# Decays that carry the key factors in the exponent, chunks inverted in batches of four and six, and merges in three groups

## The chip, the cores and the metric

The kernel runs on one core of one Trainium2 chip. A core has TensorE (PE in the profile), VectorE (DVE), ScalarE (ACT), GpSimd (POOL) and SyncE (SP), which issues most of the loads and stores; ACT and POOL issue some as well. Each engine works through its own instructions in the order in which they stand. The metric is the time of one execution in microseconds (us), measured on the device, as the median of repeated runs.

## What is computed

The kernel computes one layer of a diffusion block over 256 context tokens and 1024 latent tokens of width 1024: norms with learned modulation, one input projection, two groups of heads, an output projection, and a feed-forward layer. The change lies in the first group, four heads of a gated delta rule, run once forwards and once backwards. What it computes for each chunk of tokens is this part of the reference, cut:

```python
G = jnp.cumsum(gc, axis=-1)
diff = G[..., :, None] - G[..., None, :]
decay = jnp.where(incl, jnp.exp(jnp.where(incl, diff, 0.0)), 0.0)
kb = kc * bc[..., None]
A = jnp.where(strict, jnp.einsum('nbhid,nbhjd->nbhij', kb, kc) * decay, 0.0)
rhs = jnp.concatenate([vc * bc[..., None], kb * jnp.exp(G)[..., None]], axis=-1)
sol = lax.linalg.triangular_solve(A + jnp.eye(CHUNK, dtype=A.dtype), rhs,
                                  left_side=True, lower=True, unit_diagonal=True)
qk = jnp.einsum('nbhid,nbhjd->nbhij', qc, kc) * decay
```

Here g is the log of the decay, `bc` is a sigmoid of a projection (beta), and k has been normalized to length one. A scan over the chunks follows, in which each step uses the solution, `qk` and the state.

## The kernel before

The kernel works with chunks of 128 tokens: ten of them (`TT`), chunks 0 and 1 being context. All matrix products in 32 bits are run as three matmuls of split operands (`whi`, `wlo`, `hhi`, `hlo`). Stages in the order of time:

- Up to about 275 us: modulation, the first token-major projections (`token_major`, whose three matmuls stand at L341 to L343 and are called tm here), and the convolution blocks of k and q (`conv_block`, L576 to L578).
- The decay stage, about 280 to 363 us: `pre(t)` for each chunk. PE makes the products of keys with keys (`kk`, L665) and with queries (`kq`, L675) and transposes the queries (`qt`, L670); ACT squares the transposed queries for their norms (L672). For each of the two directions a row of cumulated decays is loaded over all partitions (`gw`, L678). POOL adds a column to each head's 128x128 block (`e`, L683, with `nG`, the negated cumulated decay), and replaces what lies on the wrong side of the diagonal (L685). ACT takes the exponential of all four heads at once (L687). DVE multiplies `kk` and `kq` by it and by a column `ab`, which is beta over the squared key norm, head by head (`ut`, L695; `sp`, L697). `ut` is stored to DRAM (`un`), `sp` as well. `gw` has two buffers, `e` two, `sp` two, `ut` two. Convolution blocks of V fill PE in between.
- V's transposes (`vT`, L820), from which ACT makes scaled copies (`vt`, L823, one buffer) and stores them (ACT's own DMA queue), 12 stores in all.
- `invert(b)`: for the chunks of batch b, the 32x32 diagonal blocks of the triangular matrices are loaded one block to a partition (`yr`), and inverted by DVE in 31 steps of two instructions (L730, L732); the result is transposed (`XT`, L734) and stored (`xd`, L736). The batches are `[0,1,2,9]`, `[3,8,4,7]` and `[5,6]`.
- `merge(b)`: builds the inverse of the whole 128x128 matrix from its blocks. `blocks(b)` loads `un` to a tile `U` (L747), and the inverted blocks into `U` (L751) and into `t64` (L752, `t` in the trace). PE then multiplies 32x32 blocks (L771, L778, L781; `m`) and 64x64 blocks (L794, L798). The result is stored for the scan. tm matmuls of three groups (z, rq, rk) lie between these steps.
- From 582 us: the rest of the scan with the retention heads, the output projection (to about 735 us), and the feed-forward layer.

The order of each engine's instructions is set before the kernel runs, by a scheduler that simulates times and takes ready instructions by a priority, which goes by the place in the code; so one engine's order mixes stages. What SP issues is in one line, and an instruction in it that waits holds up all behind it. Tiles live in pools: a pool that is opened where another was closed uses its memory and waits for its last readers. The pool `rp` of the tile `rope` lies where `cv`, the pool of V's convolution, was:

```python
        close(CV)
        checkpoint("v")
        RP = pool("rp", side="right")
        rope = RP.tile([P, TT, P], F32, tag="rope", name="rope")
        GM = pool("gm")
        for t in BATCH[2]:
            pre(t)
        checkpoint("pre2")
        merge(0)
        SY.dma_start(rope, ap["rope"])
```

## Time and profile before

| | |
|---|---|
| median of 3 runs | 1484.18 us (1483.59 to 1484.78) |
| the profiled execution's own time | 1486.29 us |
| its span, first to last instruction | 1484.5 us |
| mean granted clock of TensorE | 0.977 of full speed |
| PE busy | 1406.9 us, 95% |
| DVE busy | 974.2 us, 66% |
| POOL busy | 628.4 us, 42% |
| ACT busy | 604.9 us, 41% |

The shares are means over stages with different limits, so that a stage has to be looked at by itself. A row of a window gives each engine's busy time in a stretch. The granted clock is a mean over the stretch of two levels, 2.4 GHz (1.00) and 1.2 GHz. Matmul durations in the trace overlap: of back-to-back matmuls the distance between their starts tells what one costs.

### The profile page before, as it was taken

The page shows a single profiled execution, that of the slowest core. Times are in us where ns is not written, and L with a number is a line of the kernel's source. Part 1 is how long each engine was busy: PE and PEld are TensorE (multiplying, and loading weights), DVE is VectorE, ACT ScalarE, POOL GpSimd, SP SyncE. Part 2 cuts the span into 40 slices and gives each one's busy share as a digit, 9 for nine tenths or more (in the row PEclk, how much of TensorE's full clock was granted, in tenths as well). Part 3 has the DMA queues.
Part 4 walks back from the last instruction along what each step waited for, and adds up shares of the span by engine and source line. Part 5 has one row for each costly group of instructions (what it writes and reads, how often), then busy time and mean ns, then how long its engine had stood idle before and what let it go on. Part 6 is the DMA issues. An engine that isn't in the chain of part 4 may idle for free.

```text
span 1484.5 us, 24226 instructions
## 1 busy us (share of the span) xinstructions
PE 1406.9 (95%) x8919; PEld 1206.4 (81%) x8919; DVE 974.2 (66%) x1938; ACT 604.9 (41%) x1268; POOL 628.4 (42%) x581
## 2 busy tenths in 40 slices
PE   7999999987988899999799899999999999999997
PEld 2798888976878899999688688777888888788886
DVE  6566788269868345689767876656555555657486
ACT  5543564375541121245534533323333333444454
POOL 0120011377124343234134689899555553335321
PEclk9999999998999899999899999999999999999999
DMA  8536686578597755996633265765222242776863
GB/s 321 208 99 212 188 250 202 165 233 273 175 266 204 248 186 205 414 361 221 204 114 114 85 207 215 258 243 183 106 107 107 106 144 79 237 278 190 308 204 114
DMA packets 176567, 298.16 MB, mean 201 GB/s; under 512 B 43496, under 2 KB 93880, under 8 KB 172096
## 3 DMA queue, kind: packets, MB, share of 16 engines
q1 hardware_dynamic: 124896, 253.17, 49.5%
q10 hardware_dynamic: 49072, 35.83, 7.7%
q0 software_dynamic: 2480, 7.60, 1.4%
q8 instruction: 70, 1.15, 0.3%
q14 instruction: 49, 0.40, 0.1%
HBM read 206.60 MB, written 89.96 MB: 200 GB/s over the span
## 4 chain that ended last, share of the span: by engine, by line
PE 42%; POOL 4%; DMA 2%; DVE 1%; issue 1%; ACT 0%; SPq 0%; POOLq 0%; ACTq 0%; DVEq 0%
PE ffn L1306 7%; PE ffn L1305 7%; PE ffn L1304 7%; PE fo L1432 4%; PE fo L1430 4%; PE fo L1431 4%; PE op L1163 2%; PE op L1164 2%; PE op L1165 2%; DMA wd<-tw 1%; POOL ws L1277 1%; POOL tw L1358 1%; POOL tw L1357 1%; DVE wlo L315 1%; POOL tw L1359 0%
## 5 line engine op out<-in xcount | busy, mean ns | idle before, releaser
L341 PE MATMUL tm<-whi,hhi 128*128 128x256 f32 (+1 forms) x704 | 201.1, 289 | 5.6 <-ACT xa L354 1.6
L342 PE MATMUL tm<-wlo,hhi 128*128 128x256 f32 (+1 forms) x704 | 201.3, 288 | 0.6 <-DVE wlo L315 0.6
L343 PE MATMUL tm<-whi,hlo 128*128 128x256 f32 (+1 forms) x704 | 199.2, 287 | 0.0
L341 PEld LDWEIGHTS tm<-whi,hhi 128*128 128x128 f32 x704 | 134.0, 191 | 10.0 <-ACT xa L354 2.4
L1304 PE MATMUL ffn<-t,whi 128*128 128x512 f32 x352 | 137.0, 390 | 2.0 <-ACT whi L314 2.0
L1306 PE MATMUL ffn<-t,wlo 128*128 128x512 f32 x352 | 137.1, 390 | 1.5 <-DVE wlo L315 1.5
L1305 PE MATMUL ffn<-t,whi 128*128 128x512 f32 x352 | 137.0, 389 | 0.0
L314 ACT ACTIVATE whi<-wraw 128x512 fp32r<-128x512 f32 (+2 forms) x98 | 75.2, 771 | 151.4 <-PE ffn L1305 80.5
L342 PEld LDWEIGHTS tm<-wlo,hhi 128*128 128x128 f32 x704 | 134.6, 191 | 1.8 <-DVE wlo L315 1.1
L343 PEld LDWEIGHTS tm<-whi,hlo 128*128 128x128 f32 x704 | 134.1, 192 | 1.8 <-issue 0.9
L314 ACT ACTIVATE whi<-ws 128x512 fp32r<-128x512 f32 x88 | 55.6, 632 | 175.4 <-PE ffn L1305 121.6
L315 DVE TENSOR_TENSOR wlo<-ws,whi 128x512 fp32r<-128x512 f32 x88 | 94.3, 1073 | 47.7 <-ACT whi L314 47.5
L1430 PE MATMUL fo<-whi,ahi 128*128 128x512 f32 x308 | 119.3, 390 | 1.3 <-ACT ahi L314 1.3
L1431 PE MATMUL fo<-wlo,ahi 128*128 128x512 f32 x308 | 119.9, 389 | 0.0
L1432 PE MATMUL fo<-whi,alo 128*128 128x512 f32 x308 | 119.0, 390 | 0.0
L315 DVE TENSOR_TENSOR wlo<-wraw,whi 128x512 fp32r<-128x512 f32 (+2 forms) x92 | 100.3, 1092 | 25.0 <-ACT whi L314 25.0
L1304 PE MATMUL ffn<-b,whi 128*128 128x512 f32 x264 | 103.9, 393 | 4.1 <-ACT whi L314 4.1
L1306 PE MATMUL ffn<-b,wlo 128*128 128x512 f32 x264 | 103.9, 394 | 1.1 <-DVE wlo L315 1.1
L1305 PE MATMUL ffn<-b,whi 128*128 128x512 f32 x264 | 103.8, 393 | 0.0
L576 PE MATMUL b<-hhi,whi 128*128 128x512 f32 (+1 forms) x256 | 96.3, 376 | 1.5 <-ACT y L580 1.5
L578 PE MATMUL b<-hhi,wlo 128*128 128x512 f32 (+1 forms) x256 | 95.2, 372 | 0.0
L577 PE MATMUL b<-hlo,whi 128*128 128x512 f32 (+1 forms) x256 | 94.9, 371 | 0.0
(427 smaller groups left out, 3494.6 us busy)
## 6 DMA issues: line engine op xcount, KB each, us to landing
adaw<-ada_w SPq DMA_DIRECT2D x48, 512.0 KB, 4.6
pk<-sd SPq DMA_DIRECT2D x16, 1536.0 KB, 10.1
wraw<-wfi SPq DMA_DIRECT2D x44, 512.0 KB, 4.0
ar<-ad SPq DMA_DIRECT2D x33, 512.0 KB, 4.7
w<-wfo SPq DMA_DIRECT2D x22, 512.0 KB, 4.6
wd<-tw SPq DMA_DIRECT2D x11, 1024.0 KB, 4.8
ad<-act SPq DMA_DIRECT2D x20, 512.0 KB, 3.0
raw<-wd SPq DMA_DIRECT2D x20, 512.0 KB, 4.9
```

What stands on the lines that cost most here:

```text
L314: S.activation(hi, raw, AF.Copy)
L315: e.tensor_tensor(lo, raw, hi.bitcast(F32), ALU.subtract)
L341: T.matmul(o, hhi[:, k, tsl], whi[:, k % 4, :], start=(k == 0), stop=False)
L342: T.matmul(o, hhi[:, k, tsl], wlo[:, k % 4, :], start=False, stop=False)
L343: T.matmul(o, hlo[:, k, tsl], whi[:, k % 4, :], start=False, stop=(k == KT - 1))
L576: T.matmul(o, whi[:, k, :], hh, start=(k == 0), stop=False)
L1304: T.matmul(o, whi[:, k, :], xhi(xn, slice(0, 4), k), start=(first and k == 0), stop=False, **kw)
L1305: T.matmul(o, whi[:, k, :], xlo(xn, slice(0, 4), k), start=False, stop=False, **kw)
L1306: T.matmul(o, wlo[:, k, :], xhi(xn, slice(0, 4), k), start=False, stop=(k == 3), **kw)
L1430: T.matmul(po[g][i], ahi[:, ts], whi, start=(j == 0 and not kw), stop=False, **kw)
L1431: T.matmul(po[g][i], ahi[:, ts], wlo, start=False, stop=False, **kw)
L1432: T.matmul(po[g][i], alo[:, ts], whi, start=False, stop=(j == FH - 1), **kw)
```

## The change

Four parts are changed.

1. The exponent. The column that is added to the cumulated decay now contains the log of beta and the negated log of the squared key norm too, so that `ab` is in the exponential. The log of beta comes from `softplus` on twice the width; the log of the key norms from a new function `log` of 22 DVE instructions on 128x40 numbers. POOL's four additions per chunk and direction go: the select reads `gw` itself, and ACT's exponential adds the column as its bias, one head at a time. `ut` and `sp` become one product each over all four heads.
2. The batches are `[0, 1, 2, 9]` and `[3, 8, 4, 7, 5, 6]`. In the second there are 192 blocks, two to a partition on 96 partitions, so that each of the 62 instructions covers twice the elements. `yr`, `L` and `X` have one buffer, and `XT` uses that of `yr`. The loads of `yr` come in eight pieces where there were four.
3. The merges run over chunks 0 to 3 of the first batch, 0 to 2 of the second and 3 to 5 of the second. `U` and `t64` have two buffers; the loads of inverted blocks are 16 pieces a group where there were eight. All ten `pre` stand ahead of V's stage. The pool of `pre` is opened last and closed before the merges' pool opens.
4. The loads of V's convolution weights, their splits and the two evictions of each bank get the priority of the beginning of the decay stage (`mark`), and all four weight splits are on DVE, where two were on POOL.

```diff
+FAR = -1e30
...
+    def as_of(mark):
+
+        return tc.high_priority(offset=tc.cur_priority - mark) if mark is not None else nullcontext()
...
+    def log(pl, x, n, tag):
...
+        V.tensor_scalar(i, x.bitcast(I32), 23, None, ALU.logical_shift_right)
+        V.tensor_copy(e, i)
...
+        for k in (13, 11, 9, 7, 5, 3):
+            V.scalar_tensor_tensor(a, a, 1.0 / k, q, ALU.add, ALU.mult)
+        V.scalar_tensor_tensor(a, a, 1.0, f, ALU.add, ALU.mult)
...
+        V.scalar_tensor_tensor(a, e, 0.693359375, a, ALU.mult, ALU.add)
+        return a
...
-        av = AB.tile([P, TT * 8], F32, tag="av", name="av")
-        V.tensor_tensor(av.rearrange("p (t c) -> p t c", c=8), xa[:, :, 0:8],
-                        bc(small["dtb"], [P, TT, 8], 1), ALU.add)
+        av = AB.tile([P, 2, TT * 8], F32, tag="av", name="av")
+        av3 = av.rearrange("p a (t c) -> p a t c", c=8)
+        V.tensor_tensor(av3[:, 0], xa[:, :, 0:8], bc(small["dtb"], [P, TT, 8], 1), ALU.add)
+        V.tensor_scalar(av3[:, 1], xa[:, :, 8:16], -1.0, None, ALU.mult)
         S.activation(nA, small["alog"], AF.Exp)
         V.tensor_scalar(nA, nA, -1.0, None, ALU.mult)
-        sp = softplus(AB, av, TT * 8, "sp")
+        sp = softplus(AB, av.rearrange("p a n -> p (a n)"), 2 * TT * 8, "sp")
+
+        lnb = GS.tile([P, TT, 2, H], F32, tag="lnb", name="lnb")
+        V.tensor_scalar(lnb.rearrange("p t d h -> p (t d h)"), sp[:, TT * 8:], -1.0, None, ALU.mult)
+        sp = sp[:, :TT * 8]
...
-        def conv_block(b, y, lat):
-
-            whi, wlo = weights(ap["wg"][b], [KT, P], G if b % 2 else V, W, SY if b in (4, 5) else S)
+        def conv_block(b, y, lat, mark=None):
+
+            with as_of(mark):
+                whi, wlo = weights(ap["wg"][b], [KT, P], G if b % 2 and mark is None else V, W, SY if b in (4, 5) else S)
...
-                S.activation(u[:, c0:c0 + n], o, AF.Copy)
-                S.activation(y[:, c0:c0 + n], o, AF.Copy, scale=cw[:, b, 2:3])
+                with as_of(mark):
+                    S.activation(u[:, c0:c0 + n], o, AF.Copy)
+                    S.activation(y[:, c0:c0 + n], o, AF.Copy, scale=cw[:, b, 2:3])
...
+        lnk = log(GS, nkf, TT * H, "ln").rearrange("p (t h) -> p t h", h=H)
+        nG4 = sm["nG"].rearrange("p (t d h) -> p t d h", d=2, h=H)
+        V.tensor_tensor(lnb, lnb, bc(lnk, [P, TT, 2, H], 2), ALU.subtract)
+        V.tensor_tensor(nG4, nG4, lnb, ALU.add)
...
-        GP = pool("gp")
         GU = pool("gu")
         GI = pool("gi")
-
-        BATCH = [[0,1,2,9],[3,8,4,7],[5,6]]
+        GP = pool("gp")
+
+        BATCH = [[0, 1, 2, 9], [3, 8, 4, 7, 5, 6]]
...
                 e = GP.tile([P, H, P], F32, tag="e", name="e", bufs=2)
+                sg = 1 if d == 0 else -1
+                G.affine_select(out=e, in_=gw, compare_op=ALU.is_ge, fill=FAR, base=0,
+                                pattern=[[0, H], [sg, P]], channel_multiplier=-sg)
                 for h in range(H):
                     col = t * 8 + d * 4 + h
-                    G.tensor_scalar(e[:, h, :], gw[:, h, :], sm["nG"][:, col:col + 1], 1.0, ALU.add, ALU.mult)
-                sg = 1 if d == 0 else -1
-                G.affine_select(out=e, in_=e, compare_op=ALU.is_ge, fill=NEG, base=0,
-                                pattern=[[0, H], [sg, P]], channel_multiplier=-sg)
-                S.activation(e, e, AF.Exp)
+                    S.activation(e[:, h, :], e[:, h, :], AF.Exp, bias=sm["nG"][:, col:col + 1])
                 if t >= 2:
                     sp = GP.tile([P, 2, H, P], F32, tag="sp", name="sp", bufs=2)
                 ut = GU.tile([P, H, P], F32, tag="ut", name="ut", bufs=2)
-                for h in range(H):
-                    col = t * 8 + d * 4 + h
-                    hs = slice(h * P, (h + 1) * P)
-                    abc_ = sm["ab"][:, col:col + 1]
-                    V.scalar_tensor_tensor(ut[:, h, :], pk[:, hs], abc_, e[:, h, :], ALU.mult, ALU.mult)
-                    if t >= 2:
-                        V.scalar_tensor_tensor(sp[:, 0, h, :], pq[:, hs], abc_, e[:, h, :], ALU.mult, ALU.mult)
+                V.tensor_tensor(ut.rearrange("p h i -> p (h i)"), pk, e.rearrange("p h i -> p (h i)"), ALU.mult)
+                if t >= 2:
+                    V.tensor_tensor(sp[:, 0].rearrange("p h i -> p (h i)"), pq, e.rearrange("p h i -> p (h i)"), ALU.mult)
                 SY.dma_start(un[b][:, 1 - d, c * H:(c + 1) * H, :], ut)
...
-            nc_ = len(BATCH[b])
-            nu = nc_ * H
-            nb = 4 * nu
+            nb = 4 * len(BATCH[b]) * H
+            two = 2 * nb > P
+            rows, E = (nb, 2) if two else (2 * nb, 1)
             xd = xds[b] = dr.tile([4 * nb, 1024], F32, tag="xd%d" % b, name="xd%d" % b)
-            yr = GI.tile([P, 1024], F32, tag="yr", name="yr", bufs=1)
+            new = lambda tag, n=2048: GI.tile([P, n], F32, tag=tag, name=tag, bufs=1)
+            yr, L, X = new("yr"), new("L"), new("X")
+
+            def part(t, e):
+
+                return t[:nb, e * 1024:e * 1024 + 1024] if two else t[e * nb:(e + 1) * nb, :1024]
+
             for k in range(4):
-                SY.dma_start(yr[k:2 * nb:4].rearrange("r (i j) -> r i j", j=32),
-                             un[b][q32[k]].rearrange("i e u j -> (e u) i j")[:, :, q32[k]])
...
+                for e in range(2):
+                    SY.dma_start(part(yr, e)[k::4].rearrange("r (i j) -> r i j", j=32),
+                                 un[b][q32[k], e].rearrange("i u j -> u i j")[:, :, q32[k]])
...
+            m = lambda t: t[:rows, :E * 1024].rearrange("p (e i j) -> p e i j", e=E, j=32)
             for j in range(31):
                 n = 31 - j
...
+                tmp = GI.tile([P, 512], F32, tag="tmp", name="tmp", bufs=2)
+                sh = [rows, E, n, j + 1]
+                t3 = tmp[:rows, :E * n * (j + 1)].rearrange("p (e i c) -> p e i c", e=E, c=j + 1)
+                V.tensor_tensor(t3, bc(m(L)[:, :, j + 1:, j], sh, 3), bc(m(X)[:, :, j, :j + 1], sh, 2), ALU.mult)
+                xs = m(X)[:, :, j + 1:, :j + 1]
                 V.tensor_tensor(xs, xs, t3, ALU.subtract)
...
+            XT = new("yr")
+            V.tensor_copy(m(XT).rearrange("p e i j -> p (e i) j"), m(X).rearrange("p e i j -> p e j i"))
+            for i, x in enumerate((part(X, 0), part(XT, 1), part(X, 1), part(XT, 0))):
...
-        def blocks(b):
-
-            nu = len(BATCH[b]) * H
-            nb = 4 * nu
-
...
-            uu = GM.tile([P, 2, len(BATCH[b]), H, P], F32, tag="U", name="U%d" % b, bufs=1)
-            SY.dma_start(uu.rearrange("p e c h j -> p e (c h) j"), un[b])
-            tt = GM.tile([P, 2, nu, 64], F32, tag="t64", name="t64", bufs=1)
+        def blocks(b, c0, nc_):
+
+            nu = nc_ * H
+            us = slice(c0 * H, c0 * H + nu)
+            xv = xds[b].rearrange("(s u b) (i j) -> s b i u j", s=4, b=4, j=32)
+            uu = GM.tile([P, 2, nc_, H, P], F32, tag="U", name="U", bufs=2)
+            u4 = uu.rearrange("p e c h j -> p e (c h) j")
+            SY.dma_start(u4, un[b][:, :, us])
+            tt = GM.tile([P, 2, nu, 64], F32, tag="t64", name="t64", bufs=2)
             G.memset(tt, 0.0)
             for k in range(4):
-                SY.dma_start(uu[q32[k]].rearrange("p e c h j -> p (e c h) j")[:, :, q32[k]], blk(xds[b][:2 * nb], k))
-                SY.dma_start(tt[q32[k]].rearrange("p e u j -> p (e u) j")[:, :, (k % 2) * 32:(k % 2) * 32 + 32],
-                             blk(xds[b][2 * nb:], k))
+                for e in range(2):
+                    SY.dma_start(u4[q32[k], e][:, :, q32[k]], xv[e, k][:, us])
+                    SY.dma_start(tt[q32[k], e][:, :, (k % 2) * 32:(k % 2) * 32 + 32], xv[2 + e, k][:, us])
             return uu, [uu[:, 1 - d] for d in range(2)], [tt[:, d] for d in range(2)]
 
-        def merge(b):
-
-            uu, ub, t64 = blocks(b)
-            nu = len(BATCH[b]) * H
+        def merge(b, c0, nc_):
+
+            uu, ub, t64 = blocks(b, c0, nc_)
...
+        mark = tc.cur_priority
         solve(0)
         solve(1)
         for h in range(H):
             y = newy()
-            conv_block(8 + h, y, False)
+            conv_block(8 + h, y, False, mark)
...
+        close(GP)
         GM = pool("gm")
-        for t in BATCH[2]:
-            pre(t)
-        checkpoint("pre2")
-        merge(0)
+        merge(0, 0, 4)
         SY.dma_start(rope, ap["rope"])
-        invert(2)
-        checkpoint("inv2")
-        merge(1)
-        merge(2)
+        merge(1, 0, 3)
+        merge(1, 3, 3)
...
         close(GU)
-        close(GP)
```

In the order of POOL the additions (`TENSOR_SCALAR`, L683) stood between the selects and the products for `sp`. Before, at the beginning of the decay stage:

```order
13 L683 TENSOR_SCALAR e<-gw,nG 128x128 x8
14 L685 AFFINE_SELECT e<-e 128x512 x2
15 L683 TENSOR_SCALAR e<-gw,nG 128x128 x8
16 L685 AFFINE_SELECT e<-e 128x512 x2
17 L683 TENSOR_SCALAR e<-gw,nG 128x128 x8
18 L685 AFFINE_SELECT e<-e 128x512
19 L701 TENSOR_TENSOR sp<-gw,qc 128x512
```

In the changed kernel, at the same place:

```order
14 L728 AFFINE_SELECT e<-gw 128x512 x4
15 L742 TENSOR_TENSOR sp<-gw,qc 128x512 x2
16 L728 AFFINE_SELECT e<-gw 128x512
17 L742 TENSOR_TENSOR sp<-gw,qc 128x512
18 L728 AFFINE_SELECT e<-gw 128x512
19 L742 TENSOR_TENSOR sp<-gw,qc 128x512
```

Only the selects and the products are left there.

On SP, from the store of the first batch's inverted blocks to the loads of the first merge (the numbers in names tell the batches apart: in before `un_2860` is the first, `un_2861` the second, `un_2862` the third). Before:

```order
132 L736 DMA xd_3091<-X 64x1024 x2
133 L736 DMA xd_3091<-XT 64x1024 x2
134 L698 DMA un_2862<-ut 128x512 x2
135 L747 DMA U_4267<-un_2860 128x4096
136 L834 DMA rope<-rope 128x1280
137 L702 DMA sd<-sp 128x1024
138 L752 DMA t_4269<-xd_3091 32x32x32 x2
139 L702 DMA sd<-sp 128x1024
140 L678 DMA gw<-grow_d 128x512
141 L752 DMA t_4269<-xd_3091 32x32x32 x2
142 L751 DMA U_4267<-xd_3091 32x32x32 x2
```

In the changed kernel, where `un_2893` is the second batch's:

```order
139 L782 DMA xd_3078<-X 64x1024 x2
140 L782 DMA xd_3078<-yr 64x1024 x2
141 L764 DMA yr<-un_2893 24x32x32 x8
142 L791 DMA U<-un_2892 128x4096
143 L878 DMA rope<-rope 128x1280
144 L791 DMA U<-un_2893 128x2x1536
145 L797 DMA t_4181<-xd_3078 32x16x32 x8
146 L796 DMA U<-xd_3078 32x16x32 x8
147 L782 DMA xd_3547<-X 96x1024 x2
```

The stores and loads of chunks 5 and 6 (`ut`, `sp`, `gw`) are gone from between; the load of the second group's `U` stands between `rope` and the first merge's `t`.

On PE the first merge ends with 64x64 products, and in before the second merge's first products (32x32) came 126 tm matmuls later. In the changed kernel they follow directly:

```order
2262 L377 MATMUL tm<-whi,hlo 128x256
2263 L843 MATMUL m_4409<-U,xt_4410 64x64 x16
2264 L815 MATMUL m_4471<-t_4453,U 32x32 x48
2265 L375 MATMUL tm<-whi,hhi 128x256
2266 L376 MATMUL tm<-wlo,hhi 128x256
```

The tm matmuls that lay between now stand behind. Ahead of the first merge there are 312 tm matmuls in the changed kernel where there were 360.

## Rows read from the trace of the kernel before

**Rows 1.** Windows: stretch; PE, PEld, DVE, ACT, POOL busy (count); clock, DMA share, GB/s.

```profile
280.00:300.00 20.00, 20.00 (x122) 17.65 (x122) 12.41 (x26) 10.65 (x23) 12.06 (x21) 1.00 0.47 156
300.00:320.00 20.00, 18.75 (x109) 15.90 (x108) 13.94 (x37) 12.90 (x25) 16.70 (x21) 1.00 0.70 243
320.00:340.00 20.00, 16.68 (x85) 14.88 (x84) 16.42 (x44) 14.27 (x33) 15.10 (x22) 0.83 0.85 269
340.00:360.00 20.00, 11.96 (x84) 10.82 (x82) 18.26 (x50) 12.69 (x30) 15.41 (x26) 0.86 0.83 287
360.00:380.00 20.00, 18.23 (x96) 15.34 (x97) 17.96 (x35) 11.51 (x27) 5.86 (x8) 0.80 0.65 175
...
480.00:500.00 20.00, 14.14 (x287) 13.26 (x286) 7.92 (x24) 3.42 (x6) 4.71 (x11) 0.74 0.71 236
```

**Rows 2.** Groups by line and shape, 240 to 520: busy, mean ns | idle before, releasers.

```profile
L683 POOL TENSOR_SCALAR e<-gw,nG 128x128 f32<-128x128 f32 x80 | 37.9, 490 | 55.5 <-DMA gw<-grow_d 20.8 <-DVE ut L695 15.9 <-DVE sp L697 10.9
...
L695 DVE SCALAR_TENSOR_TENSOR ut<-kk,ab,e 128x128 f32<-128x128 f32 x80 | 23.8, 342 | 38.0 <-ACT e L687 38.0
...
L687 ACT ACTIVATE e<-e 128x512 f32<-128x512 f32 x20 | 12.3, 625 | 4.3 <-POOL e L685 4.1
...
L672 ACT ACTIVATE qt<-qt 128x128 f32<-128x128 f32 x32 | 8.5, 265 | 1.6 <-PE qt L670 0.8 <-ACT qt L672 0.2
...
L672 ACT ACTIVATION_READ_ACCUMULATOR qt<-qt 128x1 f32 x32 | 6.2, 193 | 0.0
```

**Rows 3.** Timeline of DVE, 278 to 284: start, duration, instruction, [idle before].

```profile
283.16 1.12 DVE L695 SCALAR_TENSOR_TENSOR ut<-kk,ab,e 128x128 f32<-128x128 f32 x4 [23.70 <-ACT e L687]
```

**Rows 4.** Waits of PE, 275 to 590: total us, times, longest.

```profile
PE m L778 <- DMA U<-xd: 4.0, 2, 3.0
PE m L771 <- DMA t<-xd: 3.9, 3, 2.6
...
PE m L771 <- DMA U<-un: 2.2, 1, 2.2
```

**Rows 5.** Timeline of PE: first kk, two tm, first merge, dense scan.

```profile
281.89 1.05 PE L665 MATMUL kk<-kc 128*128 128x128 f32 x8
...
419.77 0.28 PE L341 MATMUL tm<-whi,hhi 128*128 128x256 f32 x1
419.89 0.28 PE L342 MATMUL tm<-wlo,hhi 128*128 128x256 f32 x1
...
423.64 0.22 PE L771 MATMUL m<-t,U 32*32 32x32 f32 x2 [2.64 <-DMA t<-xd]
...
581.59 0.61 PE L884 MATMUL Tr<-r,pk 128*128 128x128 f32 x4
```

**Rows 6.** Timeline of ACT, 560 to 720, two groups with column operands.

```profile
608.67 2.44 ACT L977 ACTIVATE XI<-dist,lgs 128x128 f32<-128x128 f32 x8
...
657.03 1.65 ACT L1058 ACTIVATE oc<-oc,nm,rry 128x128 f32<-128x128 f32 x4 [0.49 <-DVE nm L1056]
```

**Rows 7.** Timeline of ACT, V's first copies.

```profile
355.41 0.62 ACT L823 ACTIVATE vt<-vT,svy 128x128 f32<-128x128 f32 x2 [0.53 <-PE vT L820]
```

**Rows 8.** Timeline of DVE, end of the third inversion.

```profile
488.66 1.05 DVE L734 COPY XT<-X 64x1024 f32<-64x1024 f32 x1
```

**Rows 9.** Timeline of SP's queue, 385 to 520: start, issue time, DMA.

```profile
415.95 0.33 SPq L834 DMA_DIRECT2D rope<-rope  x1
...
416.86 2.20 SPq L752 DMA_DIRECT2D t<-xd  x2
...
456.62 3.99 SPq L752 DMA_DIRECT2D t<-xd  x4
464.64 0.34 SPq L747 DMA_DIRECT2D U<-un  x1
...
504.02 3.13 SPq L752 DMA_DIRECT2D t<-xd  x4
```

**Rows 10.** DMA issues, 300 to 530: count, KB each, median us to landing.

```profile
U<-un SPq DMA_DIRECT2D x2, 2048.0 KB, 9.6
```

53 lines of the change are left out of this document (30 added, 23 removed).

## The prediction

> **What bounds the kernel now.** I read the windows first: in each stretch of 20 us, how long each engine worked and at what clock TensorE ran [rows 1]. Over the whole span TensorE is busy 1406.9 of 1484.5 us, and the change leaves its matmuls as they are, so what can move is the time in which TensorE waits or runs at a lower clock. Two places lose most of it here. From 300 to 380 TensorE's busy time falls from 20.00 to 11.96 of 20 and the mean granted clock to between 0.80 and 0.86, which is a mix of the 2.4 and the 1.2 GHz level. In these stretches DVE is busy up to 18.26 of 20, POOL 15 to 17, ACT 13 to 14: this is the decay stage, `pre`, in which POOL builds an exponent, ACT takes the exponential, DVE multiplies, and the next chunk waits for the buffers. No engine is full; the ring of three is. The second place is the merges, 420 to 500, where TensorE falls to 14.14 of 20 at a clock of 0.74.
>
> Then I read what these places wait for. In the decay stage DVE's `ut` stands 38.0 us behind ACT's `e`, and POOL's `e` 55.5 us behind loads and DVE [rows 2]; the longest single wait, 23.70 us, is only the stage's beginning [rows 3]. In the merges TensorE waits for DMA: 4.0 us for `U<-xd` and 3.9 for `t<-xd`, among others [rows 4].
>
> Last I read times on the path, as I use them in the sum [rows 5]: the first kk at 281.89, the first merge matmul at 423.64, the first matmul of the dense scan at 581.59. From the first merge to the dense scan are 158.0 us. TensorE's work in it is, counted in the order, 888 tm matmuls at 0.12 us apart (two neighbours stand in the same rows), 106 us, and 25 us of merge and scan matmuls at the intervals that the trace has where nothing waits: 131 us. So 27 us are lost behind the first merge.
>
> **The change, part by part.**
>
> *The exponent.* Of POOL 80 instructions of 490 ns go, 37.9 us [rows 2]; the select stays. Of DVE 144 products of about 342 ns become 36 of 512 columns. Four small ones take 1.37 us, so a wide one is cheaper than that; I count nothing for it, as DVE then waits for ACT more. ACT pays: 20 exponentials of 128x512 at 625 ns become 80 of 128x128, each with the bias in a column. The nearest row of that shape is XI, eight with a column operand in 2.44 us, 0.305 each; the upper bound is `oc` with two column operands, four in 1.65 us, 0.41 each [rows 6]. I take XI, since one column operand is what it has too.
>
> ACT's sum in the stage: 10.65 + 12.90 + 14.27 + 12.69 = 50.5 us from 280 to 360 [rows 1], with eight of the ten chunks. Splitting the exponentials of these eight: 64 x 0.305 - 16 x 0.615 (12.3/20) = +9.7. Chunks 5 and 6, which now stand here as well: 8 squares of 0.265 + 0.193, 16 exponentials of 0.305 and 4 wide ones of 0.625, together 11.1 [rows 2, 6]. That is 71.3 us. The busiest engine of the ring got to 91% (DVE, 340 to 360), ACT to 71% [rows 1]; with POOL gone from the ring I take 88% for ACT, so 81 us. The order puts 20 convolution matmuls behind the first kk that stood ahead of it, so that the stage opens 4.6 us earlier, at about 277, and ends at 358 to 359. Bounds: 71.3 us without a gap, 349; at 71%, 378. Before, the V transposes behind it began a little before the first copy at 355.41 [rows 7]. So the stage ends no earlier, with two more chunks in it.
>
> The Trainium skill, "ScalarE: Activation LUTs", section "What ACT_TABLE_LOAD costs", gives an instruction with a per-partition bias 280 ns and 0.833 ns an element, and lets neighbours overlap by 93 ns. That is 0.387 us alone and 0.294 in a row, estimates from its figures; XI's 0.305 agrees with the second. By the first, with something between any two, ACT's sum would be 6.6 us longer and the stage would end some 7 us later, the worse half of my range.
>
> *The logarithm.* 22 small DVE instructions on 128x40 and a few more. DVE waits 23.70 us ahead of its first `ut` [rows 3], and the logarithm needs only the key norms of the stage before. It is hidden; without that cover I bound it by 26 x 0.342 = 9 us above (the small products) and nothing below, and take 0.
>
> *V's weights and evictions* go ahead in ACT's and DVE's order, and two of POOL's weight splits go to DVE. These are among the engines' sums above; I take 0, between -1 and +2.
>
> *The batches.* The third inversion disappears into the second: its XT copy at 488.66 [rows 8] was what the third merge's loads waited for, and these went out at 504.02 [rows 9]. 62 instructions of double length replace 124. It starts when before's second did and ends earlier than before's third. What is late next is the second merge's own load.
>
> *The first merge.* Its `t` loads stand on SP behind the load of `rope`, which waits until the last of V's stores has landed: copies from 355.41 on [rows 7], `rope` at 415.95, `t` from 416.86 [rows 9], first merge matmul at 423.64 [rows 5]. From the first copy to `rope` are 60.5 us for 12 stores through one buffer. Now chunks 5 and 6 no longer lie between them; I allow 4 us for that, so `rope` at 359 + 56 = 415. Behind `rope` the new order has `U<-un` of the second group, 1.5 MB, ahead of the `t` loads. 2 MB take 9.6 us [rows 10], so this one some 7. Then the loads of `t` come in eight pieces: pieces of half the size issued in 0.78 us (four in 3.13, from 504.02), whole ones in 1.0 (four in 3.99, from 456.62) [rows 9], so 6.3 to 8 us for eight. Together, partly overlapped, the first merge's data are there about 11 us behind `rope`: 426 (bounds 415 and 436). TensorE itself would be there sooner, since the order has 48 tm matmuls fewer ahead of it, 48 x 0.12 = 5.7 us; it waits for the data, and these 5.7 us of work are then still to be done. So the first merge costs 2.4 + 5.7 = 8 us.
>
> *Second and third merge.* Here the 27 us shrink. With one `U` buffer the second group's `U<-un` could go only at 464.64, behind the first merge's end [rows 9]; now it lies long before. That removes the waits of 2.2 us for `U<-un` and of 1.0 and 3.0 for `U<-xd` that TensorE had there, and the clock of 0.74 behind them (14.14 x 0.26 = 3.7) [rows 1, 4]. The third merge's loads follow at once and are hidden by tm work. What I leave: 3 us for the second eight pieces of `U<-xd` in the first merge (0 to 6), 2.5 of lower clock behind the first wait, 3 at the second merge (0 to 8; its inversion ends by about 440, and 16 pieces take 12 us more to issue), 1 at the third, 4 for the small gaps that tm has with evictions. That is 13.5 of the 27, and 13.5 are saved.
>
> *Behind it.* 8.7 us of scan work run beside tm instead of in the dense part; that saves perhaps 1.5 us of waiting there (0 to 3).
>
> **Sum.** +2.4 + 5.7 - 13.5 - 1.5 = -7 us. The profiled execution took 1486.29 us with its span of 1484.5, 2.1 above the median of 1484.18; so 1479 beside it, and **1477** by the median. A difference of 0.2%, 3 us, is about what can be told from none: below 1481.2 it is faster, above 1487.2 slower.
>
> **The rivals.**
>
> *Slower: ACT binds the decay stage.* At 0.41 us an exponential, ACT's sum is 79.7 us, and at 88% the stage ends at 368, 9 us later, 1486; at 0.305 but 71% it ends at 377, 18 later, 1495. V's first copies, the stores, `rope` and the first merge all follow by as much, since the merge waits for them. I give it 1490. It decides from the point where the V transposes begin after about 369: 10 us late eats the gain of 7 and the 3 that can be measured. For it: the ring never let ACT work above 71%. Against it: POOL leaves the ring, and ACT's waits for POOL with it.
>
> *No change: the first merge takes all.* If `U<-un` of the second group lies in front of the `t` loads with its whole 7 us and the eight pieces come behind it, 17 us pass behind `rope`, the merge starts at 432, and the sum is -1: 1483. For it: SP's queue runs in order. Against it: the loads go over the same 16 engines side by side.
>
> *A larger gain: ACT is hidden.* If POOL was what held the ring, the stage ends at 349, `rope` goes at 404, and the merge starts at 415, when TensorE gets there: 11 us more, 1466.
>
> **How the numbers follow.** Forecast (1471 to 1481) 0.44; larger gain 0.18; no change 0.18; slower 0.20. The gain's two cases make faster 0.62. The range reaches to the larger gain and to the slower case at 1490 and leaves out what lies beyond: 1463 to 1491.
>
> **What would show it.** In the profile after: the V transposes at 355 to 362, exponentials of about 0.3 us in groups of four, POOL's busy time from 300 to 360 below 10 of 20; `rope` at about 415; the first merge waiting for `t<-xd` by more than 2.6 us, 8 to 15; no wait for `U<-un` in the later merges; the dense scan at about 575. It is wrong if the transposes begin after 369 or before 350, or if the second inversion ends after 450, so that the merge behind it waits again.

## The result, and the profile of the changed kernel

| | before | changed |
|---|---|---|
| median | 1484.48 us | 1492.02 us |
| profiled execution, own time | 1486.29 us | 1492.14 us |
| span | 1484.5 us | 1490.4 us |
| mean granted clock | 0.977 | 0.973 |
| PE / DVE / ACT / POOL busy, us | 1406.9 / 974.2 / 604.9 / 628.4 | 1409.2 / 945.6 / 613.7 / 584.9 |

One of before's four executions here took 3012.29 us and stands in no comparison. The ratio is 1.0046, 95% interval 1.003 to 1.0062: slower by 7 us, where 7 us of gain were forecast. Every engine's work moved as the change says. POOL and DVE have less to do, ACT a little more.

First the windows of the changed kernel, with the columns of [rows 1]:

```profile
320.00:340.00 20.00, 16.10 (x90) 14.10 (x89) 16.24 (x27) 14.52 (x35) 7.21 (x7) 0.91 0.66 208
340.00:360.00 20.00, 14.67 (x90) 13.49 (x90) 15.29 (x23) 13.32 (x42) 8.88 (x7) 0.88 0.87 282
360.00:380.00 20.00, 13.24 (x54) 10.94 (x53) 18.70 (x44) 10.92 (x38) 6.21 (x7) 0.61 0.62 214
...
400.00:420.00 20.00, 13.42 (x102) 13.22 (x101) 11.85 (x24) 7.39 (x20) 3.14 (x2) 0.83 0.54 183
...
480.00:500.00 20.00, 20.00 (x445) 18.83 (x445) 4.95 (x15) 4.41 (x10) 5.72 (x12) 0.96 0.63 186
```

From 320 to 360 POOL's busy time is halved, ACT's is where it was, and TensorE is no better off than in [rows 1]; the stage's poor end has moved from 340 to 360 into 360 to 380, at a clock of 0.61. From 480 to 500, where before had 14.14 at 0.74, TensorE is full: the later merges do run through. New is 400 to 420, with 13.42 (before had 19.46 there).

What happened at 400 to 436 is in three timelines (start, duration, engine and line, instruction, count, and in brackets the idle time ahead of it and what ended it; "q" marks the issue of a DMA). First SP's, of the changed kernel:

```profile
407.09 0.34 SPq L791 DMA_DIRECT2D U<-un  x1
422.98 0.34 SPq L878 DMA_DIRECT2D rope<-rope  x1
423.37 0.59 SPq L791 DMA_DIRECT2D U<-un  x1
424.08 11.89 SPq L797 DMA_DIRECT2D t<-xd  x8
```

ACT's, of the same kernel:

```profile
407.33 0.38 ACTq L870 DMA_DIRECT2D sd<-vt  x1
407.75 1.06 ACT L348 ACTIVATE whi<-wraw 128x1024 fp32r<-128x1024 f32 x1 [0.45 <-ACT vt L869]
415.25 1.14 ACT L869 ACTIVATE vt<-vT,svy 128x128 f32<-128x128 f32 x4 [6.43 <-DMA sd<-vt]
416.26 0.40 ACT L536 ACTIVATE res<-tm 128x256 f32<-128x256 f32 x1
```

And TensorE's, with the first V transpose, the stall, and the first merge matmul:

```profile
368.29 0.69 PE L866 MATMUL vT<-ident,y 128*128 128x128 f32 x2 [0.48 <-ACT qt L718]
...
416.71 0.58 PE L375 MATMUL tm<-whi,hhi 128*128 128x256 f32 x1 [6.58 <-ACT res L536]
...
435.08 0.21 PE L815 MATMUL m<-t,U 32*32 32x32 f32 x2 [2.59 <-issue]
```

SP issues the first group's `U`, 2 MB, at 407.09. ACT issues one of V's last stores, 128 KB, a quarter of a microsecond later. That store lands only at 415; V's copies have one buffer, so ACT waits 6.43 us for it, with the eviction of a tm bank next in its line, and TensorE, whose tm needs the bank, stands for 6.58 us. In before the order was the other way for all but the last of the 12 stores: `U` at 405.07, that store at 407.46. There ACT had no copy left to make, but SP's `rope` waited for the store, and the first merge's `t` stands behind `rope`. A row of SP's waits in before, 403 to 425 (total, times, longest):

```profile
SPq L834 <- DMA sd<-vt: 10.2, 1, 10.2
```

In the changed kernel the chain of [rows 9] follows later by 7: `rope` at 422.98 (before 415.95), the second group's `U`, and eight pieces of `t` that take 11.89 us to issue. The first merge starts at 435.08 (before 423.64, [rows 5]).

### The profile page after: what moved, and what is told of

It is laid out like the page before. It is cut to its first block, busy times and chain, and to the rows that moved or that the text cites. A ratio compares the mean times of both kernels' runs of the same rounds, so it can differ in the third digit from the quotient of the medians.

```text
span 1490.4 us, 24085 instructions
## 1 busy us (share of the span) xinstructions
PE 1409.2 (95%) x8919; PEld 1210.6 (81%) x8919; DVE 945.6 (63%) x1795; ACT 613.7 (41%) x1327; POOL 584.9 (39%) x497
## 4 chain that ended last, share of the span: by engine, by line
PE 55%; POOL 7%; DMA 6%; issue 3%; DVE 3%; ACT 2%; SPq 0%; POOLq 0%; ACTq 0%; DVEq 0%
PE ffn L1347 6%; PE ffn L1346 6%; PE ffn L1345 6%; PE fo L1471 5%; PE fo L1473 5%; PE fo L1472 5%; PE tm L376 3%; PE tm L375 3%; PE tm L377 3%; DMA wd<-tw 2%; PE op L1204 2%; PE op L1206 2%; PE op L1205 2%; DMA sd<-vt 2%; POOL ws L1318 1%
```

## The experiments

The question was which of three things cost the 7 us and the 7 that were expected: ACT's split exponentials, the longer decay stage, or what the loads do to V's stores and to the first merge. Before took between 1484.5 and 1487.7 us on the chips that were used, so ratios to before on the same chip are compared. One thing gets in the way: an edit ahead of it can give the later, dense part of the scan a new order, and in seven of the twelve kernels up to e12 this part has one long wait which neither before nor the changed kernel has. In e5, a row of TensorE's waits from 500 to 800 (who waits, for whom: us in total, times, longest):

```profile
PE ro L1086 <- DVE nm L1097: 7.4, 1, 7.4
```

The table therefore has TensorE's busy time in two windows, 280 to 580 (where the change lies) and 580 to 760 (the dense part), beside the ratio. e2, e5, e7, e9, e10, e11, e12 and e14 have that wait, of 7.4 to 7.9 us (9.7 in e14; in e11 and e14 it is put down to a load of `vg`), and 155.6 to 159.9 us of TensorE's busy time in the second window; all others have 162.2 to 164.4. This idle time cannot simply be taken off the totals. From the last tm matmul to the last output matmul the seven with 7.4 to 7.9 take 236.8 to 239.8 us, and the changed kernel, e3, e4 and e6, which have no such wait, 238.7 to 239.9: the seven have 1458 to 1472 matmuls left there, the others 1490 to 1499. What the new order costs by itself is not separated. Before, e1, e8 and e13, which have before's batches, take 246.4 to 250.4 for 1549 to 1579. Only e14 takes longer than the kernel that it was made from: 247.1 us for 1506 matmuls, e6 239.4 for 1490. Busy time also counts what runs at the lower clock: from 280 to 580 the clock is 0.94 in before and 0.92 in the changed kernel.

| kernel | ratio to before (95%) | first V transpose | first merge | TensorE busy 280 to 580 | 580 to 760 |
|---|---|---|---|---|---|
| before | 1 | 354.9 | 423.6 | 268.0 | 164.4 |
| changed | 1.0046 (1.003 to 1.0062) | 368.3 | 435.1 | 263.4 | 164.3 |
| e1 exponent alone | 1.005 (1.0032 to 1.0068) | 358.3 | 435.3 | 261.5 | 163.7 |
| e2 batches alone | 1.0117 (1.0102 to 1.0133) | 371.4 | 441.2 | 257.3 | 159.4 |
| e3 rope apart | 0.9997 (0.9978 to 1.0016) | 361.2 | 436.0 | 267.3 | 163.3 |
| e4 rope first | 1.0078 (1.0059 to 1.0097) | 368.3 | 435.5 | 255.9 | 164.3 |
| e5 two V buffers | 1.0084 (1.0056 to 1.0113) | 367.9 | 423.9 | 262.8 | 158.8 |
| e6 both | 0.9944 (0.9926 to 0.9963) | 358.9 | 406.9 | 272.8 | 164.1 |
| e7 rows by POOL | 1.0014 (1.0 to 1.0028) | 363.3 | 436.4 | 264.2 | 159.9 |
| e8 before with both | 0.9973 (0.9953 to 0.9993) | 356.5 | 416.5 | 268.1 | 162.2 |
| e9 three buffers | 1.0053 (1.0033 to 1.0072) | 362.6 | 437.3 | 262.3 | 158.9 |
| e10 e6 and e7 | 1.0061 (1.0041 to 1.008) | 364.1 | 421.9 | 261.2 | 158.6 |
| e11 e6, old exponent | 1.0079 (1.0055 to 1.0103) | 367.3 | 421.3 | 261.6 | 159.6 |
| e12 no priority for V | 1.0057 (1.0036 to 1.0078) | 365.3 | 434.9 | 263.6 | 159.8 |
| e13 e1, two V buffers | 0.9999 (0.9981 to 1.0016) | 356.5 | 411.1 | 273.8 | 162.9 |
| e14 e6, one U | 1.0018 (1.0003 to 1.0033) | 360.8 | 409.6 | 272.1 | 155.6 |

### One part of the change at a time: e1, e2, e13

e1 puts the exponent's part alone on before: the softplus for both halves, the logarithm, and the loops of the decay stage, of which these lines are the core.

```diff
-                    G.tensor_scalar(e[:, h, :], gw[:, h, :], sm["nG"][:, col:col + 1], 1.0, ALU.add, ALU.mult)
-                S.activation(e, e, AF.Exp)
+                    S.activation(e[:, h, :], e[:, h, :], AF.Exp, bias=sm["nG"][:, col:col + 1])
```

> The kernel before with the exponent's part alone: logs in the exponent's column, no additions on POOL, 80 exponentials of 128x128 instead of 20 of 128x512, wide products on DVE; batches, merges and V's priorities as before. Theory A (the exponent's part is nearly neutral, because the decay stage is a chain of waits through loads, POOL, ACT and SP's line, and no engine's sum bounds it; the loss of the changed kernel comes from having two more chunks ahead of V's stage and from what the merges' loads do): first V transpose at 351 to 357, median 1480 to 1487. Rival B (ACT's split exponentials, 25.7 us busy instead of 12.3, are the cost): first V transpose at 360 or later, median 1489 or more.

e2 goes the other way and takes the same lines, with the logarithm, out of the changed kernel, so that the batches and merges remain.

```diff
-                    S.activation(e[:, h, :], e[:, h, :], AF.Exp, bias=sm["nG"][:, col:col + 1])
+                    G.tensor_scalar(e[:, h, :], gw[:, h, :], sm["nG"][:, col:col + 1], 1.0, ALU.add, ALU.mult)
+                S.activation(e, e, AF.Exp)
```

> The changed kernel with the exponent as it was before (additions on POOL, one exponential of 128x512, products head by head); batches of four and six, merges in three groups with two buffers and V's priorities as changed. Theory A: as slow as the changed kernel or slower, 1489 to 1497, first V transpose at 366 to 376, first merge matmul at 432 or later. Rival B: the loss is gone, 1480 to 1486, first V transpose below 362.

e1 came out as the rival had it by time, and near theory A's point by the decay stage, which ends at 358.3. A good part of the time goes elsewhere. (Its profiled execution took 1498.05 us, 7 above its own median, so its windows look worse than its usual run.) SP's timeline in e1:

```profile
404.25 0.39 SPq L781 DMA_DIRECT2D U<-un  x1
```

ACT's in e1:

```profile
404.68 0.37 ACTq L858 DMA_DIRECT2D sd<-vt  x1
...
414.14 1.14 ACT L857 ACTIVATE vt<-vT,svy 128x128 f32<-128x128 f32 x4 [9.22 <-DMA sd<-vt]
```

TensorE's in e1:

```profile
415.34 2.07 PE L704 MATMUL kk<-kc 128*128 128x128 f32 x8 [7.08 <-ACT vt L857]
```

It is the same collision in a kernel that has before's batches: `U` at 404.25, V's store at 404.68, 9.2 us of waiting on ACT and 7.1 on TensorE. So e13 gave e1 a second buffer for V's copies.

```diff
-vt = CV.tile([P, 4, P], F32, tag="vt", name="vt", bufs=1)
+vt = CV.tile([P, 4, P], F32, tag="vt", name="vt", bufs=2)
```

> The kernel of e1 (the exponent's part alone on the kernel before) with two buffers for V's copies. In e1 the first batch's U load was issued at 404.25, V's store behind it at 404.68, and TensorE waited 7.1 us for the queries' squares that stand behind V's copy on ACT. Theory D: this wait falls below 2 us, median 1482 to 1487, so that the exponent's part alone is neutral. Rival: the exponent's part costs the 7 us by itself (in the decay stage), the wait goes elsewhere: 1489 to 1494.

0.9999: with two buffers the exponent's part alone is level with before. Before with two buffers and nothing else was not run (with this edit and e3's it gains 0.27%, e8 below), so that the part by itself is neutral is likely and not shown. In e13 V's last store is issued at 389.68 and `U` at 391.62, in this order, and the wait of 7.1 us is gone. (Its profiled execution took 1479.2 us, 6 under its own median, so its windows flatter it.) e2 is slower than the changed kernel, 1.0117 to 1.0046, or 10.5 us. Its last tm matmul comes 8.6 us later (608.2 to 599.6), so most of that arises ahead of the dense part. Its first inversion is stored at 395.80, in the changed kernel at 379.63. So with ten chunks in the stage, and the order that comes with them, the exponent's part is a gain.

### Who stands first in line: e3, e4, e5, e6, e8

e3 gives `rope` a place of its own ahead of the pool of the convolutions, so that it need not wait for V's stores, and loads it ahead of the inversion's first solve.

```diff
         close(AB)
+        RP = pool("rp", side="right")
+        rope = RP.tile([P, TT, P], F32, tag="rope", name="rope")
         CV = pool("cv", side="right")
...
+        SY.dma_start(rope, ap["rope"])
         mark = tc.cur_priority
         solve(0)
...
-        RP = pool("rp", side="right")
-        rope = RP.tile([P, TT, P], F32, tag="rope", name="rope")
         close(GP)
         GM = pool("gm")
         merge(0, 0, 4)
-        SY.dma_start(rope, ap["rope"])
```

> The changed kernel with the table for the rotation in memory of its own, loaded ahead of the decay stage, so that its load no longer stands in SP's line with a wait for V's last stores. Theory C (in the changed kernel the first merge is late because its loads stand behind that load, at 422.98, and then behind the second group's U of 1.5 MB): loads of t issued by 410, first merge matmul at 415 to 422 instead of 435, median 1478 to 1486. Rival D (the DMA engines are full of the two U loads, 2 MB and 1.5 MB, and of V's stores; who stands first in line does not matter): first merge matmul at 428 to 436, TensorE waits for the evictions of tm by 5 us or more at 408 to 416, median 1488 to 1493.

e4 exchanges two lines of the changed kernel and nothing else.

```diff
-        merge(0, 0, 4)
         SY.dma_start(rope, ap["rope"])
+        merge(0, 0, 4)
```

> The changed kernel with the load of the rotation's table ahead of the first group's U in SP's line, so that both U loads (2 MB and 1.5 MB) are issued behind V's last stores and not in front of the last two. Theory D (U's 2 MB, issued at 407.09, hold up V's store of 407.33 until 415, ACT waits 6.4 us for it with an eviction of tm behind it, and TensorE waits 6.6 us): this wait falls below 2 us, V's last store goes out by 412, rope by 416, but both U loads and t then come one behind the other, first merge matmul at 430 to 438; median within 4 us of the changed kernel, 1487 to 1493. Theory C alone: TensorE's wait of 6.6 us stays, nothing changes ahead of 420.

e4 shows the collision cleanly, as its order is otherwise that of the changed kernel. With `U` issued at 418.58, behind V's last store, ACT's wait at this place is 0.36 us. ACT's timeline in e4:

```profile
410.26 0.89 ACT L869 ACTIVATE vt<-vT,svy 128x128 f32<-128x128 f32 x3 [0.36 <-DMA sd<-vt]
```

SP's timeline in e4:

```profile
418.18 0.35 SPq L877 DMA_DIRECT2D rope<-rope  x1
418.58 1.08 SPq L791 DMA_DIRECT2D U<-un  x2
419.78 16.86 SPq L797 DMA_DIRECT2D t<-xd  x8
```

TensorE's longest wait from 400 to 460 in e4 (total, times, longest):

```profile
PE m L815 <- DMA t<-xd: 9.5, 1, 9.5
```

This kernel does what theory D says up to the first merge, and its time lies above the range that was set. TensorE's 6.6 us are gone and come back as 9.5 us at the first merge, where it now waits for `t` behind 3.5 MB of `U`; the kernel is slower still. In e3 the collision stays, as expected of theory D: both `U` loads go at 406.61, ACT waits 10.87 us for V's store, TensorE 6.8. The 7 us that e3 gains on the changed kernel do not come from the first merge, which is no earlier. What is seen instead is a new order of the decay stage, which was not expected: the first kk stands at 251.7 (278.2 in the changed kernel), the V transposes at 361.2.

e5 gives V's copies a second buffer in the changed kernel, with the line of e13.

> The changed kernel with two buffers for V's scaled copies instead of one. Theory D (U's load of 2 MB, issued just ahead of one of V's last stores, makes that store land late, and with one buffer ACT waits for it with an eviction of tm behind): ACT's waits for V's stores fall from 16.8 us to below 5, TensorE's wait of 6.6 us for the eviction falls below 2, median 4 to 8 us below the changed kernel: 1484 to 1488. Rival E (the time that TensorE gains there it loses at the first merge, whose loads come no earlier, first merge matmul still at 433 to 437): median 1489 to 1493.

e6 is the changed kernel with e3's edit and e5's.

> The changed kernel with both: the rotation's table in memory of its own and two buffers for V's copies. Theory C with D: t's loads issued by 412, first merge matmul at 418 to 425, no wait above 2 us for evictions at 400 to 425; median 1472 to 1481, below the kernel before. Rival E: 1482 to 1487, because the merges' data come when they come.

e8 is before with the same two edits.

> The kernel before with the rotation's table in memory of its own and two buffers for V's copies, to see what the same two edits are worth without the change. If they only remove what the change brought in (theory D), 1480 to 1485, for before's U load went out behind all but one of V's stores; if they are worth as much to before as to the changed kernel, 1470 to 1478.

e5 misses by the mechanism too. The two buffers let V go on, `U` came forward to 399.11, and V's next to last stores again lay behind it: ACT waited 7.49 us at 409.49, and TensorE 5.2 us behind it. Its first merge starts 11 us earlier than in the changed kernel, and the kernel is none the faster. Two buffers by themselves do not cure the collision; it is gone where V's stores are issued first (e4, e6, e13). In e6 both edits together put the whole of V's stores ahead (the last copy at 387.55) and `U` and `t` behind. The second group's `U` goes out only at 407.75, behind all of `t`. SP's timeline in e6:

```profile
393.49 0.53 SPq L793 DMA_DIRECT2D U<-un  x1
394.13 8.32 SPq L799 DMA_DIRECT2D t<-xd  x4
```

And TensorE's first merge matmul in e6:

```profile
406.93 0.22 PE L817 MATMUL m<-t,U 32*32 32x32 f32 x2 [3.78 <-DMA t<-xd]
```

The first merge starts 28 us earlier than in the changed kernel, which has no long wait in the dense part either. The last merge matmul hardly moves (511.7, changed 513.1), as the second inversion is stored no earlier (444.48, 444.72). What moves is the last tm matmul, 583.1 to 599.6: from 280 to 440 TensorE is busy 140.9 us at a clock of 0.95, in the changed kernel 129.9 at 0.88, in e3 139.2 at 0.94. The whole takes 1479.04 us where before, on the same chip, took 1487.06: 0.56% below before, and the version that beats both. e8, before with both edits, gains 0.27% (0.07 to 0.47), so about half of e6's lead over before remains for the change itself. e6 moves several things at once (V's stores, the decay stage's order as in e3, and the second `U` behind `t`), and how much each is worth is not separated.

### The decay stage: e7, e9, e10, e12

e7 moves the load of the decays' rows from SP's queue to POOL's.

```diff
-                SY.dma_start(gw.rearrange("p h i -> p (h i)"),
+                G.dma_start(gw.rearrange("p h i -> p (h i)"),
```

> The changed kernel with the loads of the decay rows issued by POOL instead of SP, nothing else. Theory F (the decay stage is held by SP's line: its stores of ut wait 30.4 us for DVE, and the next decay rows are loaded only behind them): POOL's waits for gw fall from 16.2 us below 6, first V transpose at 352 to 361 instead of 368, median 4 to 10 us below the changed kernel. Rival G (what holds it is ACT's line, where evictions of V's convolution stand behind exponentials, or DVE, at 16 of 20 us): first V transpose at 365 to 372, median within 4 us of the changed kernel.

e9 gives the stage's tiles `gw`, `e` and `ut` three buffers; the line of `e` stands for the three.

```diff
-                e = GP.tile([P, H, P], F32, tag="e", name="e", bufs=2)
+                e = GP.tile([P, H, P], F32, tag="e", name="e", bufs=3)
```

> The changed kernel with three buffers instead of two for the decay rows, the exponentials and ut. Theory H (the decay stage is held by the turn of each pair of buffers, from load over select, exponentials, product on POOL and store back to the load, about 4.5 us for each of 20 turns, and no engine's sum): first V transpose at 350 to 360 instead of 368, POOL's waits for gw and SP's for ut both lower by half; median 1483 to 1489 (the collision of U's load with V's stores stays). Rival G (the order of the lines holds it: evictions behind exponentials on ACT, ut behind inversion steps and convolution taps on DVE): first V transpose at 364 to 370, median 1489 to 1495.

e12 takes the priority from V's convolutions, and with it puts two of their weight splits back on POOL.

```diff
-            conv_block(8 + h, y, False, mark)
+            conv_block(8 + h, y, False)
```

> The changed kernel without the fourth part: V's weights and evictions at their own place's priority, two weight splits on POOL again. If the priority pays for itself: TensorE waits longer for V's evictions (L621, 5.2 us in the changed kernel), median 1493 to 1500. If it is one cause of the late stage, because exponentials wait behind evictions: first V transpose before 366 and median 1486 to 1490.

e10 is e6 with e7's line.

> The kernel of e6 (rotation's table in memory of its own, two buffers for V's copies) with the decay rows' loads issued by POOL, as in e7. If both gains add up (theories D and F): 1473 to 1477. If the merges' data, which here come in the order U, U, t, hold it instead: 1477 to 1483 and the first merge matmul at 418 or later.

e7 and e9 each bring the V transposes forward by 5 to 6 us, and e12 by 3; POOL's wait for `gw` falls only from 14.8 to 11.6 (e7) and 14.3 (e9). e7 and e9 fall between the two points that had been set for each; e12's transposes come as its second case had it, its time as its first. So neither SP's line, nor the buffers, nor the priorities alone hold the stage. Each edit also gave the stage a new order, so how much each of them holds by itself is not separated. e10 did not add the gains up, and at 1497.27 us it is slower than either case had it: its order on SP is `U`, `U`, `t`, V's last stores (396.58 and 397.60) lie behind `U` (393.38) again, ACT waits 8.5 us for one of them and TensorE 7.5 us behind ACT, and the first merge starts at 421.9 and not at 406.9.

### Two last questions: e11, e14

e11 is e6 with e2's lines, the exponent made by POOL as in before.

> The kernel of e6 with the exponent as before the change: batches, merges and V's priorities as changed, rotation's table in memory of its own, two buffers for V's copies. Against e6 it tells what the exponent's part is worth once the collision is gone. Theory A' (the exponent's part frees DVE and POOL, so the second inversion ends sooner; worth about 10 us with ten chunks in the stage, as e2 against the changed kernel): 1486 to 1493, second inversion's first store after 455. If its worth was only in the collision's place: 1477 to 1482.

Against e6, e11 is 20 us slower (1.0079 to 0.9944), more than either case had it. Its last tm matmul comes at 605.0 (e6: 583.1), so the whole lag arises ahead of the dense part. Its first inversion is stored at 392.05 (e6: 377.46) and its second at 454.99 (444.48). With ten chunks the exponent's part is then worth 10 us (e2) to 20 (e11), with the new order that comes with it.

e14 is e6 with one buffer for the merges' tiles.

```diff
-            uu = GM.tile([P, 2, nc_, H, P], F32, tag="U", name="U", bufs=2)
+            uu = GM.tile([P, 2, nc_, H, P], F32, tag="U", name="U", bufs=1)
...
-            tt = GM.tile([P, 2, nu, 64], F32, tag="t64", name="t64", bufs=2)
+            tt = GM.tile([P, 2, nu, 64], F32, tag="t64", name="t64", bufs=1)
```

> The kernel of e6 with one buffer for U and one for t64, so that the second group's U load waits for the first merge's end again. If the second buffer is what lets the later merges run through (the step of the prediction that gave most of its gain): TensorE waits for DMA in the second and third merge by 6 to 12 us in all, median 1486 to 1493. If one buffer serves as well, because the second group's load then no longer stands among the first merge's loads: 1475 to 1481.

e14 came out as its first case had it: 1487.17 us, and TensorE waits for DMA by 8.5 us in the second and third merge, 3.3 for `t` and, in the third, 5.2 for `U<-xd` (waits from 430 to 535):

```profile
PE m L824 <- DMA U<-xd: 5.2, 2, 4.6
```

With one buffer the third group's `U` goes out later. SP's timelines, first of e14, then of the changed kernel:

```profile
497.81 0.56 SPq L793 DMA_DIRECT2D U<-un  x1
504.93 5.07 SPq L798 DMA_DIRECT2D U<-xd  x8
...
474.10 0.57 SPq L791 DMA_DIRECT2D U<-un  x1
482.29 3.89 SPq L796 DMA_DIRECT2D U<-xd  x8
```

The third merge's last matmul follows at 531.1 (513.1 in the changed kernel, 511.7 in e6). From 280 to 580 TensorE is busy 272.1 us in e14 and 272.8 in e6, which waits 6.1 us for `t` in its second merge; the loss of 11 us against e6 (1.0018 to 0.9944) shows behind the last tm matmul, 247.1 us to 239.4. Whether the later merge causes that or the new order does is not separated.

## Why the prediction was wrong

**The decay stage's end**: forecast 359, measured 368.3. The price of an exponential was right (25.7 us for 80, 0.32 each; 0.305 taken). The estimates from the Trainium skill, "ScalarE: Activation LUTs", section "What ACT_TABLE_LOAD costs", were 0.387 alone and 0.294 in a row; the trace agrees with both, as one alone takes 0.390 by the rows' mean and a group of four 1.28, so that they start 0.297 apart. ACT's sum was taken too high rather than too low: 64.0 us busy from 278 to 368, where 71.3 were forecast. The step that failed is "with POOL gone from the ring I take 88% for ACT". Over the stage ACT got to 71%, which was its best window in before (its mean from 280 to 360 was 63%). Taking POOL's additions out did not shorten the ring. Waits in the changed kernel, 278 to 372 (total, times, longest):

```profile
ACT e L732 <- POOL e L728: 21.4, 10, 5.4
POOL sp L742 <- ACT gw L741: 21.1, 10, 4.9
...
POOL e L728 <- DMA gw<-grow_d: 14.8, 6, 7.3
...
SPq L739 <- DVE ut L736: 27.7, 15, 5.6
```

In before, from 240 to 520, ACT waited 20.9 us for POOL's additions. Now POOL has half the work, and waits 21.1 us for ACT and 14.8 for loads which stand on SP behind stores that wait 27.7 us for DVE. A chunk takes 9.0 us of the stage, ((368.3 - 278.2) / 10), as it took 9.1 before ((354.9 - 281.9) / 8). Other kernels have nearly the same turn: 9.3 in e1, which has the new exponent and eight chunks ahead of V's stage ((358.3 - 283.7) / 8), and 9.5 in e2, which keeps POOL's additions and has ten ((371.4 - 276.5) / 10). What sets it stays open: e7, e9 and e12 each take off a part. The transposes did not begin after 369, but nearly: what I had named as the slower rival's point was all but reached, by its second way (ACT at 71% of the stage), though with less ACT work than it had.

**The first merge**: forecast 426, measured 435. `rope` was forecast 56 us behind the stage's end and came 54.7 behind it; from `rope` to the merge 11 were forecast and 12.1 measured. So the whole of the 9 us is the stage's. But inside those 54.7 us lies the stall that the prediction did not have at all: it never asked what the load of 2 MB does to a store that ACT waits for. I had counted TensorE as waiting anyway until 426, "it waits for the data"; it then stood at 410 to 417 for the eviction, and worked its tm off later, and met its first merge without any wait for `t`, where 8 to 15 us had been announced. e4 shows that the stall by itself, once taken away, is lost again at the merge. In e6, where V's stores, `U` and `t` all come earlier, the kernel is faster.

**Behind the first merge**: here lies the rest of the miss, and the term that was mis-sized is the 27 us. The sum had 5.7 us of tm more and 13.5 and 1.5 of losses less, so that the way from the first merge to the output would be 9.3 us shorter. From the first merge to the last output matmul it took 407.0 us before (423.64 to 830.68) and 403.3 now (435.08 to 838.36), 3.8 shorter. Up to the last tm matmul, before and then changed, with the columns of [rows 1]:

```profile
423.64:581.47 157.83, 144.97 (x2103) 140.46 (x2104) 86.04 (x247) 31.25 (x48) 59.77 (x112) 0.95 0.67 213
...
435.08:599.60 164.52, 157.14 (x2231) 153.23 (x2232) 66.74 (x187) 30.09 (x51) 53.23 (x104) 0.97 0.63 201
```

By idle time and clock before lost 12.9 + 7.9 = 20.8 us here (157.83 - 144.97, and 5% of the stretch for the clock of 0.95, an estimate), and not the 27 of the prediction; the changed kernel loses 7.4 + 4.9 = 12.3 by the same count. What was left, 13.5, was about right; what it was taken from was too large. Some 8.5 us were saved and not 13.5. The mechanism was borne out: in the changed kernel no row from 420 to 590 has TensorE waiting for DMA, the second `U` lies ahead of the first merge, and with one buffer the waits come back in the third merge (e14).

**The logarithm, the priorities**: taken at 0; in the changed kernel the logarithm's last instruction stands at 258.4 and no engine waits for it, and e12 without the priorities reaches its last tm matmul within 2 us of the changed kernel (597.9 to 599.6).

**The dense part**: 1.5 us of gain forecast, none seen: behind the last tm matmul TensorE idles 15.6 us before and 15.7 now.

Together: the first merge came 11.4 us later where 2.4 were forecast (9.0 more), the way to the last output matmul was 3.8 shorter where 9.3 were forecast (5.5 more), and the feed-forward layer behind it took 1.8 less (652.0 to 653.8). The span grew by 5.9 where 7 of gain were forecast; these three, 9.0 + 5.5 - 1.8 = 12.7, make up the 12.9 between.

The rival "no change" had the `U` load in front of `t`, and e4, where 3.5 MB of `U` stand there, shows that cost: TensorE waits 9.5 us for `t`. What no rival had was that the load stands in front of V's stores as well.

## What to carry to other kernels

Before moving a large load forward, look at which small stores are issued beside it on other queues and who waits for them: here 2 MB ahead of one 128 KB store stopped TensorE through ACT's line. Taking work off an engine of a ring helps only if the ring's turn gets shorter by it: here 38 us less for POOL left the turn at 9.0 us. Look at what the ring would wait for next, and count it by its time for one turn. And when a scheduler sets the order, compare two kernels stretch by stretch, between the same two matmuls, before comparing their totals: an edit here brought a wait of 7 us into a part that it did not touch, and busy time in a fixed window hid how much work was left there.

## What the runs showed of the hardware

A small store that is issued behind a large load on another queue landed late here. V's store of 128 KB, issued 0.24 us behind the load of 2 MB, took until 415 to land, some 8 us, where the median of such stores in before was 4.6 (3.0 for those of 256 KB). In e4, with the load issued behind V's stores, ACT goes on 1.8 us after the same store was issued (408.42 to 410.26). Behind 3.5 MB (e3) ACT waited 10.9 us for it. The windows of the changed kernel at this place have the DMA engines at 1.01:

```profile
408.00:412.00 4.00, 2.14 (x19) 1.94 (x17) 3.25 (x5) 0.81 (x1) 1.61 (x2) 1.00 1.01 355
412.00:416.00 4.00, 0.00 (x0) 0.00 (x0) 0.00 (x0) 0.76 (x3) 0.00 (x0) 0.66 0.51 202
```

TensorE also has idle times that end with "issue", nothing that the profile names: 3.4 us at 449.67 and 3.1 at 475.91 in the changed kernel, in the middle of the merges' small matmuls. One packet of the instruction queue, 0.02 MB, lies in 446 to 448, within the first, and one in 472 to 474, ahead of the second; but such packets lie at other places too (452 to 454, 460 to 462) where TensorE does not stop. Whether these are waits for code was not tried.
